# Chunk products of w_ada one at a time, in wider and even intervals, in a diffusion layer on one core

## The chip, the core and the metric

The kernel runs on one core of a Trainium2 chip. The metric is device time in microseconds (us), the median over several executions, less being better. TensorE (PE) multiplies, VectorE (DVE) and ScalarE (ACT) do elementwise work, GpSimd (POOL) helps, and SyncE (SP) issues most of the DMAs. Each engine works through its instructions in the order in which the program hands them over, and waits on semaphores of the others.

## What is computed

One layer of a diffusion backbone with 256 latent tokens, 256 context tokens and a model width of 2048, all in float32. Cut to what matters here:

```python
mod = silu(c) @ w_ada + b_ada          # w_ada is 2048 x 12288
sh_a, sc_a, gt_a, sh_f, sc_f, gt_f = split(mod, 6)
h = rms_norm(x, g_attn) * (1 + sc_a) + sh_a
o = hybrid_mixer(h, hc, w_in, w_out, ...)   # four head groups, one output projection
x = x + gt_a * o
h = rms_norm(x, g_ffn) * (1 + sc_f) + sh_f
x = x + gt_f * swiglu(h, ffn_wg, ffn_wu, ffn_wd)
return rms_norm(x, g_final)
```

The six parts of `mod` are called segments 0 to 5. Segments 0 and 1 (first norm) are needed at the start, segment 2 (gate of the mixer) when the output projection's first sums are added to x, segments 3 and 4 (second norm) after the output projection, and segment 5 (gate of the feed-forward part) late.

## The kernel before, in words

Weights are streamed once, as tiles of 128 rows by 512 columns. `stream_raw` (line 123) issues one DMA on SP for each tile into a ring of eight buffers named raw (`RAW`, line 133). `split` (line 136) makes of each tile two parts whose products TensorE adds: ScalarE casts the upper part (whi, line 142), VectorE subtracts to get the rest (wlo, line 145); each part has a ring of six buffers (`WB`, line 132), that is, three pairs of tiles. `mm3s` (lines 165, 166 and 168) does the three products. A raw buffer is free again when VectorE has read it.

Segments 0 and 1 are multiplied on TensorE (`ada_pe`, line 284; loads on line 203, products on line 301). Segments 2 to 5 go through `ada_block` (line 369): for each block of 512 columns, of which a segment has four, a running sum ada_acc (128 x 512) takes 16 chunks of 128 rows of w_ada. The first is scaled by ScalarE (line 378), each of the others is multiplied by a number of each partition and added by one scalar_tensor_tensor on VectorE (line 380). Then TensorE transposes the sum in four pieces (line 385), and VectorE reduces them to columns and adds the bias (lines 388, 389, for segment 4 also 391): these are called a block's tail. A step of the block handles two chunks; its load is one DMA of two chunks (`ada_raw`, line 279, on SP; `gate_raw`, line 1076, on POOL) or two DMAs into the raw ring that the weights use (`stream_raw`).

What goes between the large products is ordered by a planner written by hand (`Side`, line 32). It has a clock, `now`, in estimated us of TensorE's work, and tasks in lanes. `pump(cost)` is called after each batch of weight products (1.3 for six products of 512 columns, 2.6 for twelve): it moves the clock and lets each lane take the steps that are ready, one a lane and task in a pass, as long as the clock has not moved by more than the cost again. `finish` steps until given tasks are through. The w_ada blocks are the lane "gate", one block at a time; a block's next step is ready at `due`:

```python
due[0] = max(due[0] + gap, side.now - 4 * gap)
yield 0.0, max(0.0, due[0] - side.now)
```

so a late lane may catch up by four steps. The gaps are 7.0 and 3.0 units for two chunks of segment 2 during the w_in stages (lines 547, 550), 3.6 and 2.8 in the attention part (lines 688, 689) and 6.0 for segment 5 (line 1081).

The attention part, from line 688, has in order: projections for two head groups (`proj` pumps 1.3 for each token tile and pair of weight tiles: ML_CQ and DF_Q with two token tiles, 20.8 units each; ML_CKV with four tiles of 320 columns, 26.0; DF_K and DF_V with four, 41.6 each), twelve `attend` heads at 4.36 units each in between, `mla_up` (18.2), evacuations of the projections, and `gq_prep`. Line 933 needs segment 2. The output projection (lines 960 to 970) pumps 2.6 for each of 24 pairs of tiles; the four `diff` heads (6.17 units each, line 890) run beside it. Lines 971 and 972 finish these heads and the blocks of segments 3 and 4; the last quarter of the output projection and the second norm follow.

Of the kernel before, what the change touches and what calls it, by code (L numbers as in the profile page):

```python
# [10 lines left out]
F32 = mybir.dt.float32  # L11
# [6 lines left out]
P = 128  # L18
D = 2048
# [68 lines left out]
def hybrid_dit_kernel(ctx: ExitStack, tc: tile.TileContext, a, out):  # L88
# [187 lines left out]
    scg = const.tile([P, KC, 2], F32, name="scg")  # L276
    sha = const.tile([P, KC, 2], F32, name="sha")

    def ada_raw(src, shape):
        raw = sb0.tile(shape, F32, name="araw", tag="araw", bufs=4)  # L280
        sp.dma_start(raw, src)
        return raw

    def ada_pe(pr, raws=None, per=4, wait=0.0):

# [80 lines left out]

    due = [0.0]

    def ada_block(seg, nb, gap, load, fetched=None):
        c0 = seg * D + nb * 512  # L370
        acc_ = stream.tile([P, 512], F32, name="ada_acc", bufs=2)
        for k2 in range(8):
            raw = fetched(nb, k2) if fetched else load(ada_rows[:, 2 * k2:2 * k2 + 2, c0:c0 + 512], [P, 2, 512])
            for kk in range(2):
                kc = 2 * k2 + kk
                part = raw[kk] if isinstance(raw, list) else raw[:, kk, :]
                if kc == 0:
                    act.activation(acc_, part, AF.Copy, scale=cs[:, 0, 0:1])
                else:
                    dve.scalar_tensor_tensor(out=acc_, in0=part, scalar=cs[:, 0, kc:kc + 1], in1=acc_, op0=ALU.mult, op1=ALU.add)  # L380
            due[0] = max(due[0] + gap, side.now - 4 * gap)
            yield 0.0, max(0.0, due[0] - side.now)
        ps = misc()
        for j in range(4):
            pe.transpose(ps[:, tsl(j)], acc_[:, tsl(j)], ident)  # L385
        k4 = slice(4 * nb, 4 * nb + 4)
        base = colA1 if seg == 4 else colA
        dve.tensor_reduce(out=mcol[seg][:, k4], in_=ps.rearrange("p (j n) -> p j n", j=4), axis=AX.X, op=ALU.add)
        dve.tensor_tensor(out=mcol[seg][:, k4], in0=mcol[seg][:, k4], in1=base[:, seg * 16 + 4 * nb:seg * 16 + 4 * nb + 4], op=ALU.add)
        if seg == 4:  # L390
            dve.tensor_tensor(out=mcol[4][:, k4], in0=mcol[4][:, k4], in1=colB[:, 16 + 4 * nb:20 + 4 * nb], op=ALU.mult)
        yield 0.3, 0.0

    def add_ada(seg, gap, load, nbs=range(4), ahead=0):
        due[0] = side.now
        order = [(nb, k2) for nb in nbs for k2 in range(8)]
        held = {}

        def fetched(nb, k2):

            i = order.index((nb, k2))
            for nb_, k_ in order[i:i + ahead + 1]:
                if (nb_, k_) not in held:
                    c0 = seg * D + nb_ * 512
                    held[nb_, k_] = load(ada_rows[:, 2 * k_:2 * k_ + 2, c0:c0 + 512], [P, 2, 512])
            return held[nb, k2]

        return [side.add(ada_block(seg, nb, gap, load, fetched), lane="gate", width=1) for nb in nbs]

    parts = [[0], [1], [2, 3], [4, 5], [6, 7]]  # L410

# [126 lines left out]
    for gi, prs in enumerate(parts):  # L538
# [5 lines left out]
                    nxt[-1]["ready"] = side.now + 8.0  # L544
        if gi == 2:
            made = prepare()
            gate_tasks = add_ada(2, 7.0, ada_raw, (0, 1))
        if gi == len(parts) - 1:
            keep(*made)
            gate_tasks += add_ada(2, 3.0, ada_raw, (2,))  # L550
        if gi == 0:
            first_group()
        else:
# [131 lines left out]
        pool.dma_start(g, gd.partition_broadcast(P))  # L685
        return g

    gate_tasks = add_ada(2, 3.6, stream_raw, (3,))
    mod_tasks = add_ada(4, 3.6, stream_raw) + add_ada(3, 2.8, stream_raw)

    act.activation(na_qT, na_qT, AF.Copy, scale=128.0 ** -0.5)
    sc_mm = plain_score(na_qT, na_kT, lambda h: h)
# [380 lines left out]

    groups = [(0, 4), (4, 8), (8, 11)]

    def gate_raw(src, shape):
        raw = ff.tile(shape, F32, name="graw", bufs=4)
        pool.dma_start(raw, src)
        return raw

    gate_f = add_ada(5, 6.0, gate_raw, ahead=3)
    gfin = ff.tile([P, D], F32, name="gfin")
    pool.dma_start(gfin, a["g_final"].partition_broadcast(P))
    for gi, (f0, f1) in enumerate(groups):
# [135 lines left out]
```

## Time and profile before

| what | us |
|---|---|
| median of 3 executions | 1363.53 (1361.96 to 1364.54) |
| the profiled execution's own time | 1367.65 |
| its span from the first to the last instruction | 1365.9 |
| TensorE busy in it | 1333.8 (98%) |
| VectorE busy in it | 915.1 (67%) |
| ScalarE busy in it | 624.9 (46%) |

The profile is one execution. A line of a timeline has the start and the length in us, the engine (PE products, PEld weight loads, a "q" for its sequencer), the line of the kernel, the operation, output<-inputs, and a count of like instructions that were merged; in brackets stands how long the engine was idle before it and what released it. A line of waits says who waited for whom, the total in us, the number of times and the longest. A line of windows has, after the stretch and its length, the busy us and the number of instructions of each engine, the granted clock of TensorE as a share of 2.4 GHz, the DMA share and GB/s.

### The profile page before, as it was taken

What the parts mean: (1) busy time and instruction counts of PE and PEld (TensorE: products, weight loads), DVE (VectorE), ACT (ScalarE), POOL (GpSimd) and SP (SyncE); (2) the same over time, 40 slices, a digit from 0 to 9 for tenths busy, and PEclk for the clock granted to TensorE, in tenths of its full rate; (3) what the DMA queues carried; (4) which work ended last, traced back from release to release, by engine and by line L of the source; (5) the groups of instructions that cost most, each with busy time, mean ns of one, the idle gap of its engine ahead of it and who ended that gap; (6) DMA issues with size and microseconds to landing.
All of it is one profiled execution on the core that took longest, in us unless ns stands there. A gap on an engine that the chain in (4) does not pass through costs nothing.

```text
span 1365.9 us, 20914 instructions
## 1 busy us (share of the span) xinstructions
PE 1333.8 (98%) x7082; PEld 1085.5 (79%) x7082; DVE 915.1 (67%) x1623; ACT 624.9 (46%) x1183; POOL 55.0 (4%) x78
## 2 busy tenths in 40 slices
PE   6999999999999999999999999999999999999997
PEld 4788888778876777777888888888888888888886
DVE  4587789988678747878895854445545566555565
ACT  5432243654334435557444444444444444444453
POOL 1100000100000000000220000000000000000000
PEclk9999999999999999999999999999999999999999
DMA  9999997586677756455997755665656665666553
GB/s 367 348 349 330 324 356 215 164 269 205 198 246 261 240 172 213 137 180 163 365 385 262 248 184 192 194 191 188 197 184 190 219 193 186 202 189 191 190 177 131
DMA packets 186687, 313.87 MB, mean 230 GB/s; under 512 B 21171, under 2 KB 61141, under 8 KB 185429
## 3 DMA queue, kind: packets, MB, share of 16 engines
q1 hardware_dynamic: 177568, 285.28, 64.0%
q0 software_dynamic: 5664, 24.14, 4.6%
q10 hardware_dynamic: 3348, 3.13, 0.8%
q8 instruction: 55, 0.90, 0.3%
q14 instruction: 52, 0.42, 0.1%
HBM read 310.36 MB, written 2.11 MB: 229 GB/s over the span
## 4 chain that ended last, share of the span: by engine, by line
PE 68%; DVE 1%; ACT 1%; DMA 0%; issue 0%; POOL 0%; POOLq 0%; DVEq 0%; SPq 0%; ACTq 0%
PE acc L165 21%; PE acc L168 21%; PE acc L166 21%; PE m L1069 1%; PE m L607 1%; PE m L862 1%; PE m L861 1%; PE m L913 1%; PE m L897 1%; PE m L658 1%; PE m L165 0%; PE m L166 0%; PE m L168 0%; ACT whi L142 0%; PE m L385 0%
## 5 line engine op out<-in xcount | busy, mean ns | idle before, releaser
L145 DVE TENSOR_TENSOR wlo<-raw,whi 128x512 fp32r<-128x512 f32 (+1 forms) x764 | 492.1, 681 | 319.5 <-ACT whi L142 314.5
L142 ACT CAST whi<-raw 128x512 fp32r<-128x512 f32 (+1 forms) x764 | 436.8, 615 | 552.5 <-PE acc L166 471.2
L165 PE MATMUL acc<-whi,h_hi 128*128 128x512 f32 x704 | 275.1, 391 | 0.7 <-ACT h_hi L1013 0.7
L166 PE MATMUL acc<-whi,h_lo 128*128 128x512 f32 x704 | 274.2, 390 | 0.4 <-DVE h_lo L1014 0.4
L168 PE MATMUL acc<-wlo,h_hi 128*128 128x512 f32 x704 | 190.7, 390 | 0.1
L165 PE MATMUL acc<-whi,h 128*128 128x512 f32 (+1 forms) x416 | 162.0, 393 | 1.3 <-ACT tok L791 0.5
L166 PE MATMUL acc<-whi,h 128*128 128x512 f32 (+1 forms) x416 | 157.7, 381 | 0.0
L168 PEld LDWEIGHTS acc<-wlo,h_hi 128*128 128x128 f32 x704 | 132.1, 188 | 28.4 <-DVE wlo L145 0.9
L165 PEld LDWEIGHTS acc<-whi,h_hi 128*128 128x128 f32 x704 | 132.2, 188 | 27.9 <-ACT h_hi L1013 1.1
L166 PEld LDWEIGHTS acc<-whi,h_lo 128*128 128x128 f32 x704 | 132.2, 188 | 27.8 <-DVE h_lo L1014 0.7
L165 PE MATMUL acc<-whi,ah 128*128 128x512 f32 (+1 forms) x364 | 139.0, 383 | 0.0
L166 PE MATMUL acc<-whi,al 128*128 128x512 f32 (+1 forms) x364 | 138.6, 382 | 0.0
L168 PE MATMUL acc<-wlo,h 128*128 128x512 f32 (+1 forms) x416 | 115.2, 381 | 2.0 <-DVE wlo L145 1.8
L380 DVE SCALAR_TENSOR_TENSOR ada_acc<-raw,cs,ada_acc 128x512 f32<-128x512 f32 x135 | 101.0, 748 | 22.6 <-DMA raw<-in_w_ada_dram 20.8
L168 PE MATMUL acc<-wlo,ah 128*128 128x512 f32 (+1 forms) x364 | 96.2, 382 | 0.0
L165 PEld LDWEIGHTS acc<-whi,h 128*128 128x128 f32 x416 | 78.3, 189 | 19.6 <-issue 4.0
L168 PEld LDWEIGHTS acc<-wlo,h 128*128 128x128 f32 x416 | 76.0, 188 | 17.8 <-DVE wlo L145 4.1
L166 PEld LDWEIGHTS acc<-whi,h 128*128 128x128 f32 x416 | 78.4, 188 | 13.7 <-issue 1.5
L165 PEld LDWEIGHTS acc<-whi,ah 128*128 128x128 f32 x364 | 68.4, 188 | 13.3
L166 PEld LDWEIGHTS acc<-whi,al 128*128 128x128 f32 x364 | 68.4, 188 | 13.2
L168 PEld LDWEIGHTS acc<-wlo,ah 128*128 128x128 f32 x364 | 67.6, 188 | 13.3
L165 PE MATMUL acc<-whi,o_hi 128*128 128x512 f32 x128 | 51.1, 401 | 1.1 <-ACT whi L142 0.8
(233 smaller groups left out, 1347.9 us busy)
## 6 DMA issues: line engine op xcount, KB each, us to landing
raw<-in_ffn_wg_dram SPq DMA_DIRECT2D x176, 256.0 KB, 2.8
raw<-in_ffn_wu_dram SPq DMA_DIRECT2D x176, 256.0 KB, 2.8
raw<-in_ffn_wd_dram SPq DMA_DIRECT2D x176, 256.0 KB, 3.7
raw<-in_w_in_dram SPq DMA_DIRECT2D x144, 256.0 KB, 4.8
raw<-in_w_ada_dram SPq DMA_DIRECT2D x144, 256.0 KB, 3.5
araw<-in_w_ada_dram SPq DMA_DIRECT2D x128, 256.0 KB, 5.2
raw<-in_w_out_dram SPq DMA_DIRECT2D x64, 256.0 KB, 3.4
graw<-in_w_ada_dram POOLq DMA_DIRECT2D x32, 512.0 KB, 6.4
```

Source lines behind the costliest of these rows:

```text
L142: act.copy(hi, raw_)
L145: dve.tensor_tensor(out=lo, in0=raw_, in1=hi.bitcast(F32), op=ALU.subtract)
L165: pe.matmul(dst, lhsT=l[0], rhs=r[0], start=start, stop=False)
L166: pe.matmul(dst, lhsT=l[0 if w_left else 1], rhs=r[1 if w_left else 0], start=False, stop=False)
L168: pe.matmul(dst, lhsT=l[1 if w_left else 0], rhs=r[0 if w_left else 1], start=False, stop=stop)
L380: dve.scalar_tensor_tensor(out=acc_, in0=part, scalar=cs[:, 0, kc:kc + 1], in1=acc_, op0=ALU.mult, op1=ALU.add)
L607: pe.transpose(ps[:, tsl(j)], src[:, tsl(j)], ident)
L658: pe.matmul(o[:, :S], lhsT=vt(kc)[:, v0:v0 + P], rhs=pT[:, kc, :], start=(kc == 0), stop=(kc == 3))
L861: pe.matmul(sc, lhsT=ml_qT[:, h, tsl(t)], rhs=ml_kT[:, h, :], start=True, stop=False)
L862: pe.matmul(sc, lhsT=qpeT[hb, h // 2, tsl(t)], rhs=kpeT[hb, :], start=False, stop=True)
L897: pe.matmul(sc, lhsT=df_qT[hb, h, tsl(t)], rhs=df_kT[h // 2][hb, h % 2, :], start=True, stop=True)
L913: pe.matmul(o[:, tsl(t)], lhsT=pT[:, kc, tsl(t)], rhs=vt[:, kc, tsl(h)], start=(kc == 0), stop=(kc == 3))
```

## The change

Each step of a block now handles one chunk, and a wait stands between the two chunks of a load as well. The gap is given for each block and for one chunk. Where the old gaps are halved (segment 2 in the w_in stages, segment 5, the last block of segment 2) the mean rate is the old one; segments 4 and 3 go from 3.6 and 2.8 units for two chunks to 2.2 for one. A late lane catches up by one chunk's gap instead of four steps. In the attention part a step loads its one chunk (one DMA, as before); elsewhere the load of two chunks stays. All blocks of that part share one call. The core of the diff:

```diff
-    def ada_block(seg, nb, gap, load, fetched=None):
-        c0 = seg * D + nb * 512
+    def ada_block(seg, nb, gap, fetched, per):
         acc_ = stream.tile([P, 512], F32, name="ada_acc", bufs=2)
-        for k2 in range(8):
-            raw = fetched(nb, k2) if fetched else load(ada_rows[:, 2 * k2:2 * k2 + 2, c0:c0 + 512], [P, 2, 512])
-            for kk in range(2):
-                kc = 2 * k2 + kk
-                part = raw[kk] if isinstance(raw, list) else raw[:, kk, :]
+        for k0 in range(0, KC, per):
+            for kk, part in enumerate(fetched(seg, nb, k0)):
+                kc = k0 + kk
                 if kc == 0:
                     act.activation(acc_, part, AF.Copy, scale=cs[:, 0, 0:1])
                 else:
                     dve.scalar_tensor_tensor(out=acc_, in0=part, scalar=cs[:, 0, kc:kc + 1], in1=acc_, op0=ALU.mult, op1=ALU.add)
-            due[0] = max(due[0] + gap, side.now - 4 * gap)
+                if kk < per - 1:
+                    due[0] = max(due[0] + gap, side.now - gap)
+                    yield 0.0, max(0.0, due[0] - side.now)
+            due[0] = max(due[0] + gap, side.now - gap)
             yield 0.0, max(0.0, due[0] - side.now)
...
-            gate_tasks = add_ada(2, 7.0, ada_raw, (0, 1))
+            gate_tasks = add_ada([(2, 0, 3.5), (2, 1, 3.5)], ada_raw)
...
-            gate_tasks += add_ada(2, 3.0, ada_raw, (2,))
+            gate_tasks += add_ada([(2, 2, 1.5)], ada_raw)
...
-    gate_tasks = add_ada(2, 3.6, stream_raw, (3,))
-    mod_tasks = add_ada(4, 3.6, stream_raw) + add_ada(3, 2.8, stream_raw)
+    def head_raw(src):
+        return stream_raw(src, [P, 1, 512])
+
+    mod_tasks = add_ada([(2, 3, 1.8)] + [(4, nb, 2.2) for nb in range(4)] + [(3, nb, 2.2) for nb in range(4)], head_raw, 1)
+    gate_tasks = mod_tasks[:1]
...
-    gate_f = add_ada(5, 6.0, gate_raw, ahead=3)
+    gate_f = add_ada([(5, nb, 3.0) for nb in range(4)], gate_raw, ahead=3)
```

`add_ada` now takes a list of (segment, block, gap), and `ada_raw` and `gate_raw` hand back the two halves of their tile.

## Rows read from the trace of the kernel before

**Rows 1.** The page's first part: busy us, share of the span, instructions.

```profile
PE 1333.8 (98%) x7082; PEld 1085.5 (79%) x7082; DVE 915.1 (67%) x1623; ACT 624.9 (46%) x1183; POOL 55.0 (4%) x78
```

**Rows 2.** Windows of 25 us (columns as told above).

```profile
225.00:250.00 25.00, 25.00 (x107) 19.35 (x106) 24.36 (x58) 8.58 (x18) 2.25 (x2) 1.00 0.65 193
250.00:275.00 25.00, 25.00 (x126) 19.76 (x125) 23.84 (x62) 17.92 (x39) 3.94 (x4) 1.00 0.60 178
275.00:300.00 25.00, 23.04 (x101) 16.69 (x100) 22.43 (x42) 15.11 (x36) 1.85 (x2) 0.93 0.81 265
300.00:325.00 25.00, 23.34 (x110) 18.07 (x108) 19.73 (x38) 13.15 (x30) 0.00 (x0) 1.00 0.75 242
...
350.00:375.00 25.00, 23.84 (x142) 20.62 (x141) 15.88 (x40) 9.67 (x29) 2.16 (x4) 1.00 0.62 174
375.00:400.00 25.00, 22.97 (x118) 19.23 (x117) 16.70 (x34) 9.14 (x18) 0.00 (x0) 0.93 0.72 220
```

**Rows 3.** Waits from 276 to 291 us: total us, times, longest.

```profile
ACT whi L142 <- DMA raw<-in_w_in_dram: 7.4, 3, 3.2
...
PE m L748 <- ACT gq_kT L742: 1.9, 1, 1.9
```

**Rows 4.** Timeline from 278 to 291 us.

```profile
279.62 3.11 DVE L380 SCALAR_TENSOR_TENSOR ada_acc<-raw,cs,ada_acc 128x512 f32<-128x512 f32 x4
...
284.16 0.93 SPq L128 DMA_DIRECT2D raw<-in_w_in_dram  x2
...
285.62 0.62 ACT L142 CAST whi<-raw 128x512 fp32r<-128x512 f32 x1 [1.14 <-DMA raw<-in_w_in_dram]
286.15 0.47 ACT L742 ACTIVATE gq_kT<-m,colB 128x256 f32<-128x256 f32 x1
...
286.67 3.51 PE L748 MATMUL m<-gq_kT,qT 128*128 128x512 f32 x4 [1.91 <-ACT gq_kT L742]
...
289.19 1.38 PE L166 MATMUL acc<-whi,h 128*128 128x512 f32 x1
...
290.40 0.40 PE L165 MATMUL acc<-whi,h 128*128 128x512 f32 x1
```

**Rows 5.** Timeline of TensorE from 308 to 320 us.

```profile
310.26 1.88 PE L748 MATMUL m<-gq_kT,qT 128*128 128x512 f32 x4
...
317.13 0.63 PE L607 MATMUL m<-ident,p 128*128 128x128 f32 x4 [1.34 <-DVE p L650]
319.45 0.63 PE L607 MATMUL m<-ident,p 128*128 128x128 f32 x4 [0.32 <-DVE p L650]
```

**Rows 6.** Waits from 384 to 394 us.

```profile
ACT whi L142 <- DVE ada_acc L380: 6.2, 1, 6.2
...
PE acc L168 <- DVE wlo L145: 1.8, 1, 1.8
```

**Rows 7.** Waits of SP's DMA queue from 220 to 500 us.

```profile
SPq L128 <- DVE ada_acc L380: 57.1, 102, 3.0
```

**Rows 8.** The tile ada_acc: duration in ns (min/median/max), first and last start in us.

```profile
L380 DVE SCALAR_TENSOR_TENSOR ada_acc<-raw,cs,ada_acc x135: 730/751/756, 222.7 to 486.2; 128x512 f32<-128x512 f32 x135
...
L378 ACT ACTIVATE ada_acc<-raw,cs x9: 712/725/736, 217.7 to 463.8; 128x512 f32<-128x512 f32 x9
...
  DMA raw<-in_w_ada_dram: 26.3, 30
```

**Rows 9.** Windows: two undisturbed ones, and the attention part.

```profile
125.00:150.00 25.00, 25.00 (x239) 20.94 (x238) 20.64 (x42) 7.11 (x13) 0.00 (x0) 1.00 0.94 321
...
875.00:900.00 25.00, 25.00 (x112) 20.71 (x111) 11.77 (x19) 11.41 (x21) 0.00 (x0) 1.00 0.62 194
...
225.00:487.00 262.00, 255.19 (x1230) 201.27 (x1229) 210.49 (x419) 116.69 (x257) 10.21 (x12) 0.99 0.73 227
```

**Rows 10.** Windows: before, during and after the output projection's first three quarters.

```profile
596.00:640.00 44.00, 41.71 (x188) 31.43 (x187) 41.76 (x81) 36.30 (x78) 1.73 (x2) 1.00 0.58 181
...
487.00:507.00 20.00, 20.00 (x92) 16.57 (x91) 6.09 (x11) 6.00 (x11) 0.00 (x0) 1.00 0.39 125
507.00:596.00 89.00, 88.52 (x432) 68.70 (x431) 67.79 (x138) 49.02 (x100) 4.67 (x7) 1.00 0.52 172
```

**Rows 11.** VectorE by line, 507 to 596 us: busy us, mean ns, idle before, releasers.

```profile
L145 DVE TENSOR_TENSOR wlo<-raw,whi 128x512 fp32r<-128x512 f32 x46 | 29.8, 686 | 12.5 <-ACT whi L142 12.3 <-issue 0.2
...
L921 DVE TENSOR_SCALAR tok<-m,rstd 128x128 f32<-128x128 f32 x8 | 2.4, 347 | 3.5 <-POOL rstd L177 2.7 <-PE m L607 0.9
...
L388 DVE TENSOR_REDUCE mcol<-m 128x4 f32<-128x512 f32 x1 | 0.7, 684 | 0.0
...
L389 DVE TENSOR_TENSOR mcol<-mcol,colA 128x4 f32<-128x4 f32 x1 | 0.2, 152 | 0.0
```

**Rows 12.** The w_in stages: a wait of SP, a batch's issue and first use, its landing.

```profile
SPq L203 <- DVE ada_acc L380: 13.1, 12, 2.0
...
135.59 2.42 SPq L203 DMA_DIRECT2D araw<-in_w_ada_dram  x3
...
153.85 1.96 PE L301 MATMUL m<-araw,cs 128*32 128x128 f32 x64
...
araw<-in_w_ada_dram SPq DMA_DIRECT2D x128, 256.0 KB, 5.2
```

**Rows 13.** Segment 5: the window of its products, and the products.

```profile
656.00:774.00 118.00, 118.00 (x538) 97.89 (x537) 101.54 (x160) 56.58 (x100) 20.23 (x28) 1.00 0.89 323
...
L380 DVE SCALAR_TENSOR_TENSOR ada_acc<-graw,cs,ada_acc x60: 739/747/754, 656.9 to 773.6; 128x512 f32<-128x512 f32 x60
```

**Rows 14.** Timeline near 521 us: a softmax row's last step and its transposes.

```profile
520.38 0.75 DVE L905 SCALAR_TENSOR_TENSOR p<-p,st 128x512 f32<-128x512 f32 x1
...
521.06 1.03 PE L607 MATMUL m<-ident,p 128*128 128x128 f32 x8
```

More of the change, by code (lines that the diff above doesn't have):

```diff
@@ L277, in hybrid_dit_kernel, with ada_raw @@
     sha = const.tile([P, KC, 2], F32, name="sha")
-    def ada_raw(src, shape):
-        raw = sb0.tile(shape, F32, name="araw", tag="araw", bufs=4)
+    def ada_raw(src):
+        raw = sb0.tile([P, 2, 512], F32, name="araw", tag="araw", bufs=4)
         sp.dma_start(raw, src)
-        return raw
+        return raw[:, 0, :], raw[:, 1, :]
     def ada_pe(pr, raws=None, per=4, wait=0.0):
@@ L392, in ada_block, with add_ada, fetched @@
         yield 0.3, 0.0
-    def add_ada(seg, gap, load, nbs=range(4), ahead=0):
+    def add_ada(blocks, load, per=2, ahead=0):
         due[0] = side.now
-        order = [(nb, k2) for nb in nbs for k2 in range(8)]
+        order = [(seg, nb, k0) for seg, nb, _ in blocks for k0 in range(0, KC, per)]
         held = {}
[L399 to L408, printed above, removed]
+        def fetched(*at_):
+            i = order.index(at_)
+            for s in order[i:i + ahead + 1]:
+                if s not in held:
+                    seg, nb, k0 = s
+                    c0 = seg * D + nb * 512
+                    held[s] = load(ada_rows[:, k0:k0 + per, c0:c0 + 512])
+            return held[at_]
+        return [side.add(ada_block(seg, nb, gap, fetched, per), lane="gate", width=1) for seg, nb, gap in blocks]
     parts = [[0], [1], [2, 3], [4, 5], [6, 7]]
@@ L1074, in hybrid_dit_kernel, with gate_raw @@
     groups = [(0, 4), (4, 8), (8, 11)]
-    def gate_raw(src, shape):
-        raw = ff.tile(shape, F32, name="graw", bufs=4)
+    def gate_raw(src):
+        raw = ff.tile([P, 2, 512], F32, name="graw", bufs=4)
         pool.dma_start(raw, src)
-        return raw
-    gate_f = add_ada(5, 6.0, gate_raw, ahead=3)
+        return raw[:, 0, :], raw[:, 1, :]
+    gate_f = add_ada([(5, nb, 3.0) for nb in range(4)], gate_raw, ahead=3)
     gfin = ff.tile([P, D], F32, name="gfin")
```

## The prediction

> **What bounds the kernel now.** I read the page first, then windows of 25 us, then the waits, the timeline and the windows of the stages that the edited lane touches. On the page TensorE is busy for 98% of the span and VectorE for 67% [rows 1]; the reader is to see that TensorE is the bound as a whole and that only stretches where its busy time falls below the window can give time back. Matmul ends are modelled, so a full window hides small waits. Where the gate columns of segment 5 are multiplied, from 656 to 774 us, TensorE is busy for 118.00 of 118 us [rows 13], so nothing is to be had there. Among the windows before, three matter [rows 2]: 275 to 300 us (23.04 of 25 busy, clock 0.93), 300 to 325 (23.34) and 375 to 400 (22.97, clock 0.93). A mean of 0.93 is some 3.5 us at the lower of the two levels, which loses half of that, 1.75 us, on top of the wait; what TensorE did just before each fall was to wait for about 2 us.
>
> The waits name the culprits. Near 284 us TensorE stood 1.9 us for gq_kT from ScalarE; ScalarE was late because a weight cast ahead of it waited for a w_in load [rows 3], and the timeline shows why: four chunk products (L380) in a row, 3.11 us, held the raw buffers, and SP issued the weights between w_ada loads that waited for those buffers [rows 4]. The four score matmuls after it took 3.51 us where the same four took 1.88 later, and the next matmul 1.38 where 0.40 is usual [rows 4, 5]: 1.6 + 1.0 us from the low clock. Near 317 us TensorE waited 1.34 and 0.32 us for a softmax row that stood behind chunks in VectorE's queue [rows 5]. Near 392 us it waited 1.8 us for a wlo, whose cast had itself waited 6.2 us for a buffer that a chunk held [rows 6]. Over 220 to 500 us SP waited 102 times, 57.1 us in all, for chunk products [rows 7]. So the lane does delay TensorE, in three places.
>
> **The change, part by part.** The chunk's price stays: 135 products of 0.75 us on VectorE and 9 scalings of 0.72 on ScalarE, all between 217.7 and 486.2 us [rows 8]. The loads stay too: stream_raw already issued one 256 KB DMA per chunk, so neither SP's count nor the bytes change. What moves is when.
>
> *Where the chunks go.* The planner's own costs between lines 688 and 972 add up to 317.5: projections 150.8, out-projection 62.4, twelve attention heads 52.3, mla_up 18.2, four differential heads 24.7, evacuations and gq_prep 6.4, nine block ends 2.7. Before, the lane asks 40 x 3.6 + 32 x 2.8 = 233.6 of it, so it is through before the out-projection (the last 62.4 + 24.7 = 87.1), as the 486.2 shows. After, it asks 16 x 1.8 + 128 x 2.2 = 310.4. At the out-projection's start, at 230.4, 16 + 201.6/2.2 = 107 chunks are out and 37 are left. The intervals are even only as far as the planner's steps of 1.3 to 2.6 and its jumps of some 6 allow, so that up to three chunks still come together; and lateness over two gaps is now lost, so the lane's end slips by several units, to about the end of the out-projection; the last one or two chunks are then emitted by the finish on line 972.
>
> *Gain.* Between 222 and 487 us VectorE gets 37 fewer chunks, 27.8 us less, in single steps. The three places cost 1.9 + 1.6 + 1.0 = 4.5, then 1.7, then 1.8 + 1.75 = 3.6, together 9.8 us [rows 2 to 6]. Bounds: 0 (only fewer chunks come there, so I see nothing that adds a wait) and 9.8. I take 7.5, nearer the top, since in each place the chunks that do the holding come two to four in a row and these rows are denser there than what the new gap allows; some of it will return as shorter waits. The 1.16 us missing between 350 and 375 belong to small evacuations and stay.
>
> One reading rule could make this term larger. The trace counts 6.8 us of missing matmul time from 225 to 487 us, but 201.27 us of weight loading in 262, or 77%, against 20.71 in 25, or 83%, where TensorE runs undisturbed [rows 9]. The Trainium skill (Perfetto Trace Analysis, Identifying the Most-Contended Engine) holds that matmul busy time is a poor measure because matmuls are pipelined, and tells us to judge by the weight loads instead: by that rule up to 19 us could be had here. The attention's 512-column fp32 matmuls load few weights per microsecond, so the waits' 9.8 us are what I count.
>
> *Loss.* The out-projection runs from 507 to 596 us, 89 us for the planner's 87.1. TensorE is busy for 88.52 of it, VectorE for 67.79 [rows 10]. To that come 37 x 0.75 = 27.8 us and two more block tails of 0.68 + 0.15 [rows 11], 1.7 us: 97.2 us of VectorE work in a stage of 89. That is 8.2 too many. Waits for rstd from GpSimd, 2.7 us, stand in VectorE's order and cannot be filled [rows 11], so 10.9. The 14 us that VectorE idles between 487 and 507 [rows 10] don't help: the first reduction of each differential head waits for scores that TensorE reaches at 507, and the chunks stand behind it. What helps: wlo buffers for three pairs, 6 x 29.8/46 = 3.9 us of VectorE's work [rows 11], are a lead that it may use up. But the stage after needs that lead: from 596 to 640 us VectorE is busy for 41.76 of 44 [rows 10], so only 2.2 us are absorbed for good. 10.9 - 2.2 = 8.7, and one fall of the clock at 1.75 makes 10.5 us. Bounds: 0, because from 225 to 275 us VectorE was busy for 24.36 and 23.84 of 25 with TensorE full [rows 2], and 17: 97.2 us at the 95% that the stage after reaches is 102.4, 13.4 over, and two falls of the clock. I take 10.5, because the demand is over 100% and not only near it. A chunk may also wait for its own load, 26.3 us over 30 cases in this lane [rows 8]; where VectorE is behind, the load has landed, so I count nothing, and the cover gone it would be 37 x 30/144 x 0.88, about 7 us, inside the upper bound with the lead used up.
>
> *Gates of segment 2 during the w_in stages, and segment 5.* Cost nothing. The second half of an araw tile is now used half an interval later, so a ring slot is held up to 3.5 units longer, and SP, which waits there already (13.1 us in 12 cases [rows 12]), issues ada_load's tiles and the w_in weights queued behind them later. The cover: a batch issued from 135.59 us is first used at 153.85 [rows 12], some 18 us on, with a landing of 5.2, and the windows are full with all of it in place [rows 9]. If that cover went, each batch would cost TensorE up to 3.5 us. Segment 5 hides under 118.00 of 118 us [rows 13]; its last product is at 773.6 and its rows are wanted in the second group's evacuations, so POOL's queue has slack.
>
> Sum: -7.5 + 10.5 = +3.0 us on the profiled execution's 1367.65, 1370.7. That execution is 4.1 above the median of 1363.53, so the median becomes 1366.5.
>
> **The rivals.** *Room in the out-projection* (not slower): the chunks fall into VectorE's 21.2 idle us there, much of it waits for a cast that itself waits for TensorE (12.3 us of ScalarE's making [rows 11]), and the lead covers the rest, loss 2 us. For it: full windows at 97% load near 240 us. Against: demand over 100%, and at 521 us the softmax row that TensorE transposes is finished only as it gets there [rows 14], so one chunk ahead of it is seen at once. -7.5 + 2 = -5.5, 1358. It decides from where the added work is under the idle that can be used.
>
> *Hidden either way*: the three waits reappear from another source (casts, loads) and the out-projection copes; both terms near 2, the time stays, 1363.5. For it: VectorE was above 95% near 270 us without a loss. Against: the named waits end on chunks.
>
> *Late hand-over* (slower): the last block's transposes are emitted by line 972, ahead of the remaining w_out products in TensorE's order, and must wait for the last chunk on a VectorE that is behind by its whole excess; the norm that follows has no slack. The full excess, 13.4, plus two falls of the clock is 17; with 4 of gain, +13, 1376.5. It decides from an excess of about the lead, 4 us, at the stage's end.
>
> **How the numbers follow.** About 0.2%, 2.7 us, is what a measurement of this kernel can tell from no change. The forecast gets 0.47, of which 0.33 lies above +2.7 and 0.14 within; the first rival 0.28 (0.25 faster, 0.03 within), the second 0.13 (0.10 within, 0.03 faster), the third 0.12, slower. Faster 0.28, same 0.27, slower 0.45. Own range of the forecast: 1362 to 1372. The range of 8 in 10 goes from 1356 (gain 9.8, loss 2) to 1376.5 (the third rival).
>
> **What would show it.** Right: chunk products lie between 218 and about 600 us; the windows 275 to 300 and 375 to 400 are full at clock 1.00; VectorE is near 100% from 510 to 595, TensorE there waits for wlo or a softmax row, and the out-projection ends about 10 us later relative to its start. Wrong: no wait of TensorE on VectorE in the out-projection and a stage of 89 to 91 us, then the kernel is faster; or the waits near 284, 317 and 392 us still there, then slower by more than forecast. Segment 2 or 5 is misjudged if TensorE waits for araw or the page shows late gate rows.

## The result, and the profile after

The kernel after takes 1376.32 us, the median of four executions (1373.23 to 1378.16), beside 1363.72 us for the kernel before on the same chip: a ratio of 1.0087 [1.0070, 1.0104], slower. The forecast was 1366.5, so the sign is right and the size is not: 12.6 us were lost where 3.0 were forecast. The profiled execution has a span of 1376.2 us, 10.3 more than before; that of before took 1367.65 us, 3.9 above its median, that of after 1378.03, 1.7 above its own, so the profiles show 2.2 us less of the loss than the medians do.

The page's first part [rows 1] now reads:

```profile
PE 1338.0 (97%) x7082; PEld 1087.3 (79%) x7082; DVE 910.4 (66%) x1623; ACT 625.2 (45%) x1183; POOL 55.2 (4%) x78
```

The counts of instructions are the same. TensorE's busy time is 4.2 us more for them, the rest of the 10.3 is waiting. To see where, cut each trace at three matmuls: the first scores of the attention part (m<-kT,qT), the first scores of the differential heads (m<-df_kT,qT, where the output projection begins), and the first product of h_hi (line 165, after the second norm). Times in us; the kernels e1 to e12 are those of the next section, the column of chunks counts products and first scalings that start after the out-projection does, and the last one is of the chunk products of the attention part's lane on VectorE:

```
kernel  attention part        out-projection   rest   chunks after     VectorE idle
        from   to     length  length                  its start        before chunks
before  244.3  507.3  263.0   115.1            743.5   0               21.0
after   246.3  505.1  258.8   127.6            743.5  30               54.2
e1      244.7  509.4  264.7   123.5            744.1   6               52.8
e2      246.1  508.5  262.4   125.1            743.6  26               49.6
e3      246.4  499.5  253.1   121.5            743.5  16                0
e4      245.6  504.4  258.8   125.6            743.6  27               56.2
e5      244.6  498.9  254.3   115.0            743.4   0                0
e6      245.6  509.7  264.1   125.6            743.8  28               56.5
e7      251.5  508.8  257.3   136.6            742.8  20               48.5
e8      245.1  504.1  259.0   115.1            743.8   0               22.5
e9      248.2  505.1  256.9   128.0            743.4   -                0
e10     248.8  519.3  270.4   115.4            744.0   0               25.0
e11     245.7  513.9  268.1   115.4            743.7   0               33.6
e12     248.7  500.8  252.1   124.9            743.4   -                0
```

The attention part is 4.2 us shorter, the out-projection 12.5 longer, and the rest is the same; 2.0 us more lie before the attention part, where executions differ anyway (the thirteen runs of before beside e12 range from 1362.95 to 1368.32).

Some of both numbers is work that changed its stage. With 30 chunks the transposes of three blocks' tails came into the out-projection. Lines of TensorE and of VectorE in the kernel after, 505 to 608 us (busy us, mean ns, idle before):

```profile
L385 PE MATMUL m<-ident,ada_acc 128*128 128x128 f32 x12 | 1.8, 271 | 0.0
```

```profile
L377 DVE SCALAR_TENSOR_TENSOR ada_acc<-raw,cs,ada_acc 128x512 f32<-128x512 f32 x29 | 21.6, 744 | 5.7 <-DMA raw<-in_w_ada_dram 5.7
```

In the kernel before all 36 of these transposes lie in the attention part. Without the 1.8 us that moved, 2.4 are won and 10.7 lost. The loss is well clear of noise: the out-projection takes 115.0 to 115.4 us in all five kernels that have no chunk in it, and 121.5 to 136.6 in all others. The gain isn't: it rests on one execution of each kernel, that of before was a long one, and e8, whose median is that of the kernel before, has an attention part of 259.0.

Windows of the kernel after, with the columns of [rows 2, 10, 13]:

```profile
275.00:300.00 25.00, 23.15 (x109) 17.19 (x107) 23.14 (x44) 16.56 (x38) 1.42 (x2) 1.00 0.83 272
300.00:325.00 25.00, 24.27 (x112) 18.93 (x113) 17.00 (x33) 12.18 (x28) 0.00 (x0) 1.00 0.61 191
350.00:375.00 25.00, 22.50 (x123) 19.14 (x123) 15.23 (x40) 9.28 (x28) 2.54 (x4) 0.93 0.51 146
375.00:400.00 25.00, 25.00 (x145) 21.99 (x145) 16.16 (x31) 8.93 (x18) 0.00 (x0) 1.00 0.70 217
...
505.00:608.00 103.00, 96.08 (x450) 73.33 (x449) 88.10 (x173) 52.52 (x106) 5.40 (x7) 0.98 0.69 228
656.00:774.00 118.00, 118.00 (x534) 97.82 (x533) 93.99 (x148) 54.67 (x96) 23.70 (x33) 1.00 0.89 326
```

Of the three places of [rows 2], the window from 375 is full, and that from 300 misses 0.7 us instead of 1.7. From 275 to 300 us the clock is 1.00, but TensorE still misses 1.85 us, where it was 1.96: the wait for gq_kT is gone, and two others of 0.67 and 0.94 us came. The window from 350, which had lost 1.16 us of TensorE's time, now loses 2.5 and stands at clock 0.93. In the out-projection TensorE misses 6.9 of 103 us, and VectorE is busy for 88.10 of 103, or 86%: it is not full.

The tile ada_acc, whose rows answer to [rows 8] (the last row: idle time of its engines before it, us and times):

```profile
L377 DVE SCALAR_TENSOR_TENSOR ada_acc<-raw,cs,ada_acc x135: 727/750/755, 224.7 to 597.1; 128x512 f32<-128x512 f32 x135
...
  DMA raw<-in_w_ada_dram: 70.4, 49
```

A product costs what it did (750 ns), but VectorE and ScalarE now stand 70.4 us in 49 cases waiting for a chunk to land, where it was 26.3 in 30. Most of it lies in the attention part; of VectorE's share 5.7 us are in the out-projection (the line of L377 above). The timeline of the kernel after near 359 us shows what one such wait does:

```profile
351.98 0.54 SPq L824 DMA_DIRECT2D raw<-in_mla_wuq_dram  x1
352.58 1.08 SPq L128 DMA_DIRECT2D raw<-in_w_ada_dram  x2
...
356.98 0.75 DVE L377 SCALAR_TENSOR_TENSOR ada_acc<-raw,cs,ada_acc 128x512 f32<-128x512 f32 x1 [3.82 <-DMA raw<-in_w_ada_dram]
...
361.12 0.48 DVE L790 SCALAR_TENSOR_TENSOR tok<-acc,rstd,b_mla_gkv 128x256 f32<-128x256 f32 x1 [0.72 <-POOL rstd L177]
...
361.65 0.69 PE L609 MATMUL m<-ident,tok 128*128 128x128 f32 x2 [2.29 <-DVE tok L790]
```

SP issues the chunk's load behind weights, 4.4 us before its use; VectorE stands 3.82 us ahead of the chunk and then works without a pause through what was queued up behind it, a block's tail and a second chunk among it, before it gets to the next tokens' evacuation; TensorE waits 2.29 us for those tokens (0.31 at this place in e3, which has no chunk loads), and then runs a stretch at the lower of its two levels (the 0.93 of that window). The same happens in the out-projection near 588 us:

```profile
583.12 0.37 SPq L128 DMA_DIRECT2D raw<-in_w_ada_dram  x1
584.82 0.75 DVE L377 SCALAR_TENSOR_TENSOR ada_acc<-raw,cs,ada_acc 128x512 f32<-128x512 f32 x1 [3.34 <-DMA raw<-in_w_ada_dram]
...
590.57 0.59 PE L609 MATMUL m<-ident,tok 128*128 128x128 f32 x2 [1.85 <-DVE tok L926]
```

The costliest wait there has no chunk's load right before it. TensorE and VectorE near 534 us:

```profile
530.92 0.74 DVE L377 SCALAR_TENSOR_TENSOR ada_acc<-raw,cs,ada_acc 128x512 f32<-128x512 f32 x1
...
533.90 0.68 DVE L961 TENSOR_TENSOR tm<-acc,gate 128x512 f32<-128x512 f32 x1
...
534.57 0.67 DVE L145 TENSOR_TENSOR wlo<-raw,whi 128x512 fp32r<-128x512 f32 x1
...
536.23 0.68 DVE L145 TENSOR_TENSOR wlo<-raw,whi 128x512 fp32r<-128x512 f32 x1
536.83 0.74 DVE L910 SCALAR_TENSOR_TENSOR p<-p,st 128x512 f32<-128x512 f32 x1
...
537.72 0.63 PE L609 MATMUL m<-ident,p 128*128 128x128 f32 x4 [3.43 <-DVE p L910]
```

VectorE works without a pause from 528 to 540 us, on chunks, casts, residual sums and softmax rows in program order; the row that TensorE transposes next comes behind all of it, 3.43 us late, and a second fall of the clock follows.

### The profile page after: what moved, and what is told of

It reads as the page before. It is cut to its first block, busy times and chain, and to the rows that moved or that the text cites. A ratio compares the mean times of both kernels' runs of the same rounds, so it can differ in the third digit from the quotient of the medians.

```text
span 1376.2 us, 20896 instructions
## 1 busy us (share of the span) xinstructions
PE 1338.0 (97%) x7082; PEld 1087.3 (79%) x7082; DVE 910.4 (66%) x1623; ACT 625.2 (45%) x1183; POOL 55.2 (4%) x78
## 4 chain that ended last, share of the span: by engine, by line
PE 80%; DVE 9%; DMA 6%; issue 2%; ACT 2%; POOL 1%; SPq 0%; ACTq 0%; DVEq 0%; POOLq 0%
PE acc L165 24%; PE acc L168 24%; PE acc L166 24%; DMA raw<-in_w_ada_dram 3%; DVE wlo L145 2%; DVE ada_acc L377 2%; PE m L301 2%; DMA araw<-in_w_ada_dram 1%; DVE st L636 1%; POOL rstd L177 1%; PE m L268 1%; PE m L1074 1%; PE m L609 1%; ACT whi L142 1%; PE m L660 1%
## 5 line engine op out<-in xcount | busy, mean ns | idle before, releaser
L377 DVE SCALAR_TENSOR_TENSOR ada_acc<-raw,cs,ada_acc 128x512 f32<-128x512 f32 x135 | 100.9, 747 | 55.5 <-DMA raw<-in_w_ada_dram 52.7
```

## The experiments

Unless said otherwise each was timed against the kernel before on the same chip, and its edit is against the kernel after. The stage table above holds all their profiled executions.

**e1: the old rate in single, even steps.**

```diff
-    mod_tasks = add_ada([(2, 3, 1.8)] + [(4, nb, 2.2) for nb in range(4)] + [(3, nb, 2.2) for nb in range(4)], head_raw, 1)
+    mod_tasks = add_ada([(2, 3, 1.8)] + [(4, nb, 1.8) for nb in range(4)] + [(3, nb, 1.4) for nb in range(4)], head_raw, 1)
```

> The changed kernel with the old mean intervals in the attention part: 1.8 units a chunk for segment 4 and 1.4 for segment 3 in place of 2.2; single steps, single loads and the one-chunk catch-up stay. By the planner's clock 13 chunks are left when the output projection starts, against 37 in the changed kernel and none before. Theory A (chunks moved into the output projection cost TensorE there, since VectorE has no slack): the stage returns to about 91 us from 103 and the time to 1364 to 1367. Theory B (a chunk loaded alone, in step with its use, makes VectorE wait for its own load, wherever it stands): those waits stay near the changed kernel's 70 us and the time stays above 1370. Theory C (catching up by one chunk only): above 1370 as well, since the catch-up is unchanged.

Measured 1384.61 us, 1.0143 [1.0117, 1.0170]; its profiled execution, 1378.82 us, was the quickest of its runs, so the table shows the smaller part of its loss. Even single steps at the old rate win nothing in the attention part (264.7 us), and although only 6 chunks are left after its start the out-projection takes 123.5. The loss sits at its head, in the timeline of e1:

```profile
507.14 1.54 DVE L377 SCALAR_TENSOR_TENSOR ada_acc<-raw,cs,ada_acc 128x512 f32<-128x512 f32 x2 [2.90 <-DMA raw<-in_w_ada_dram]
...
512.03 1.12 PE L902 MATMUL m<-df_kT,qT 64*128 64x512 f32 x2 [1.47 <-DVE mcol L388]
513.98 0.75 DVE L377 SCALAR_TENSOR_TENSOR ada_acc<-raw,cs,ada_acc 128x512 f32<-128x512 f32 x1 [2.00 <-DMA raw<-in_w_ada_dram]
...
518.40 0.80 PE L166 MATMUL acc<-whi,o_lo 128*128 128x512 f32 x1 [2.09 <-DVE o_lo L952]
```

Two steps of the lane wait for their own loads ahead of work that TensorE needs. So the number of chunks in the out-projection does not set the loss by itself. Theory A failed (1364 to 1367); B and C both gave such a time. As the rate is the old one, the whole loss of e1 comes with single steps, single loads and the short catch-up.

**e2: the kernel before (chunks in pairs), at the new mean rate.**

```diff
-    mod_tasks = add_ada(4, 3.6, stream_raw) + add_ada(3, 2.8, stream_raw)
+    mod_tasks = add_ada(4, 4.4, stream_raw) + add_ada(3, 4.4, stream_raw)
```

> The kernel before with only the wider interval: 4.4 units for two chunks in segments 4 and 3 (3.6 and 2.8 before); two chunks a step, two loads a step and the catch-up of four steps stay. 34 chunks are then left at the start of the output projection. Theory A: about as slow as the changed kernel, 1372 to 1380. Theory B: 1362 to 1367, since loads still come in twos and the second chunk finds its data there. Theory C: 1362 to 1367.

Measured 1376.98 us, 1.0093 [1.0078, 1.0109], the time of the kernel after within the intervals. Theory A holds: the wider gap alone makes a loss of this size, and at this gap single steps and the shorter catch-up change little (an attention part of 258.8 against 262.4, a difference that single executions can make). At the old rate they do cost, as e1 shows and e10 and e11 show again.

**e3 and e5: no chunk loads, in the kernel after and in the kernel before.** One tile is loaded once and every chunk product of the attention part reads it. e3:

```diff
+    hraw = const.tile([P, 512], F32, name="hraw")
+    sp.dma_start(hraw, ada_rows[:, 0, 4 * D:4 * D + 512])
...
     def head_raw(src):
-        return stream_raw(src, [P, 1, 512])
+        return [hraw]
```

> The changed kernel with the loads of segments 2 (last block), 4 and 3 in the attention part left out: one chunk of w_ada is loaded once into a tile of its own and every product there takes it. All products, their order and their intervals stay; 143 DMAs of 256 KB and their places in the raw ring are gone, so these segments are not what the reference has. Theory B: the output projection's stage falls to 90 to 93 us and the time to 1357 to 1365. Theory A: VectorE's work there is unchanged, the stage stays at 98 us or more and the time above 1370.

Measured 1365.55 us, 1.0002 [0.9992, 1.0012]. e5 does the same to the kernel before (`head_raw` gives `[hraw, hraw]` to its three add_ada calls):

> The kernel before with the chunk loads of the attention part left out, as in the run without chunk loads of the changed kernel: one chunk is loaded once and every product of segments 2 (last block), 4 and 3 there takes it, so these are not the reference's; products, pairs, intervals and catch-up are as before. It is the fair partner of that run. Theory A (VectorE's work in the output projection is what costs): this kernel keeps its lead over that run, 8 us or more: 1353 to 1358. Theory B (the chunks' own loads are what costs, through the ring and SP's queue): both kernels lose the loads' harm, and what is left between them is under 4 us: 1360 to 1365.

Measured 1359.15 us, 0.9962 [0.9951, 0.9973]. The four kernels make a square:

```
                     chunks as before   chunks as after   difference
with their loads     1363.72            1376.32           +12.6
without loads        1359.15            1365.55            +6.4
the loads cost          4.6               10.8
```

Both results lie between the theories. About half of the loss is there without any load: products that moved. The other half goes with their loads, which cost 4.6 us in the old places and 10.8 in the new. The medians of the square come from different chips; by the ratios to the kernel before on the same chip the products cost 5.5 us (e3 against e5) and the loads 5.2 and 11.6, so the split stands to about 1 us. The same split shows in the out-projection: 115.0 (e5), 121.5 (e3, of which the moved transposes are 1.8), 127.6 (after). A window of each over it, up to about 25 us before its end, e5 first and e3 second:

```profile
498.90:588.00 89.10, 88.62 (x430) 68.95 (x430) 67.87 (x139) 49.02 (x100) 4.68 (x7) 1.00 0.53 172
```

```profile
499.50:596.00 96.50, 94.33 (x447) 72.89 (x447) 79.51 (x158) 52.19 (x105) 5.53 (x7) 0.98 0.49 159
```

In e3 VectorE is busy for 79.51 of 96.50 us, and still TensorE misses 2.2 us and loses some to the clock (0.98): even without loads the added products delay by their place in VectorE's order, with 18% of its time free.

One reservation holds for the whole square. The program is put in order by its builder after the planner, and an edit that takes loads away changes the order of other instructions too. At the softmax row near 534 us the kernel after has nothing between the two groups of transposes, e3 has three products there. TensorE, the kernel after first and e3 second:

```profile
533.70 0.60 PE L609 MATMUL m<-ident,p 128*128 128x128 f32 x4
537.72 0.63 PE L609 MATMUL m<-ident,p 128*128 128x128 f32 x4 [3.43 <-DVE p L910]
```

```profile
528.04 0.60 PE L609 MATMUL m<-ident,p 128*128 128x128 f32 x4
528.39 0.48 PE L165 MATMUL acc<-whi,o_hi 128*128 128x512 f32 x1
...
530.30 0.66 PE L609 MATMUL m<-ident,p 128*128 128x128 f32 x4 [0.96 <-DVE p L913]
```

So the 3.43 us are 0.96 without the loads, and part of that difference is the other order. How much of the 11 us that go with the loads is their waits, and how much the order that they bring about, no run separates.

**e4: catch-up of eight gaps** for the lane with single chunks (the same in both lines that set `due`).

```diff
-            due[0] = max(due[0] + gap, side.now - gap)
+            due[0] = max(due[0] + gap, side.now - (8 if per == 1 else 1) * gap)
```

> The changed kernel with the old catch-up in the attention part: a late lane may catch up by eight chunks (four steps of two, as before) in place of one. The wider single intervals stay; 35 chunks are left at the start of the output projection, and the lane is through 11 units before its end instead of after it. Theory C: most of the loss goes, 1363 to 1368. Theories A and B: 1372 to 1379, as only the last chunk's hand-over is gone, 1 to 2 us.

Measured 1375.11 us, 1.0077 [1.0060, 1.0093], not to be told from the kernel after: 27 chunks stay behind instead of 30. At this gap the shorter catch-up is a detail; theory C failed.

**e6 and e7: loads issued earlier.** e6 fetches two chunks ahead (`head_raw, 1, 2`). e7 does so from a ring of three of its own, with six raw buffers for the weights:

```diff
-    RAW = 8
+    RAW = 6
...
-        return stream_raw(src, [P, 1, 512])
+        raw = stream.tile([P, 512], F32, name="hraw", bufs=3)
+        sp.dma_start(raw, src[:, 0])
+        return [raw]
```

> The changed kernel with each chunk's load handed to SP two chunks earlier (still in the weights' ring of eight); products, intervals and catch-up unchanged. Theory B: VectorE's waits for chunk loads in the attention part fall from 70 us to under 30 and the time to 1362 to 1369. Theory A: the waits may fall, but the output projection stays near 103 us and the time above 1372. A third possibility: chunks that lie in the ring two steps longer leave it too short for the weights, and the time rises above 1378.

> The changed kernel with a ring of three tiles for the chunks of the attention part, loaded two chunks ahead, and six raw tiles (in place of eight) for the weights everywhere. Theory B: a chunk's load no longer waits for a weight's slot, though it still stands in SP's order; its waits fall to under 25 us and the time to 1360 to 1368, if six raw tiles are enough for the weights (seen in the feed-forward stages, where nothing else changes). Theory A: above 1372.

e6 measured 1378.75 us, 1.0107 [1.0089, 1.0124], e7 1390.18, 1.0176 [1.0145, 1.0207], over three executions; a fourth took 6397.15 us, for a reason that is not known, and is left out. VectorE still stands 56.5 and 48.5 us before chunks. Asking for a load earlier in program order doesn't bring it earlier: it waits at its place in SP's order for a buffer, and the weights behind it wait too. In e7 SP's queue waits longest, from 225 to 640 us, for these rows (as [rows 7]):

```profile
SPq L128 <- DVE wlo L145: 128.3, 122, 13.8
SPq L692 <- DVE ada_acc L377: 65.5, 94, 5.1
SPq L692 <- DMA hraw<-in_w_ada_dram: 31.3, 30, 5.1
```

In the kernel after the first two are 121.2 in 134 cases and 63.1 in 97. The chunks' own ring did not free SP of the products, and TensorE was the worse for it (136.6 us of out-projection). The weights have two buffers fewer in e7, and what those cost here was not tried by itself; in the rest, 742.8 us, they cost nothing.

**e8: one step ahead in the kernel before** (`ahead=1` for segments 4 and 3).

> The kernel before with the loads of segments 4 and 3 handed to SP one step (two chunks) ahead; everything else as before. Theory B: the waits of VectorE for chunk loads, 26 us before, fall, and the three places near 284, 317 and 392 us cost less, since the weights' loads there no longer follow a late chunk load: 1355 to 1362. If the ring is the limit and not the moment of the load: 1364 or slower. Theory A says nothing of it: 1361 to 1366.

Measured 1365.15 us, 1.0003 [0.9993, 1.0014]. No difference in the old places either: the time is that of the ring as the limit.

**e9: the loads without the products.**

```diff
-                else:
+                elif per == 2:
                     dve.scalar_tensor_tensor(out=acc_, in0=part, scalar=cs[:, 0, kc:kc + 1], in1=acc_, op0=ALU.mult, op1=ALU.add)
```

> The changed kernel with the chunk products of the attention part left out (segments 2, last block, 4 and 3: only each block's first chunk is scaled, so these segments are not the reference's); all 144 loads keep their order and intervals in SP's queue and in the raw ring. It shows what the loads cost by themselves (ring, SP's order, DMA). Theory B1 (a load costs only because VectorE stands in order before its product): time 1350 to 1360 and an output projection of 115 us from the first score product to the first feed-forward product. Theory B2 (the loads make the weights late): that stage stays above 119 us and the time above 1360.

Measured 1377.24 us, 1.0095 [1.0074, 1.0116]: as slow as the kernel after, with no product in VectorE's order. The first scaling of each block is left, on ScalarE, and the longest wait stands before one of them. Timeline of e9:

```profile
546.73 4.91 SPq L128 DMA_DIRECT2D raw<-in_w_ada_dram  x3
550.57 0.72 ACT L375 ACTIVATE ada_acc<-raw,cs 128x512 f32<-128x512 f32 x1 [6.21 <-DMA raw<-in_w_ada_dram]
...
552.74 3.92 PE L902 MATMUL m<-df_kT,qT 64*128 64x512 f32 x4 [4.57 <-ACT oT L928]
```

ScalarE stands 6.21 us for the chunk, the copy of an output row (oT) behind it comes late, and TensorE waits 4.57 us; from 549 to 560 us its granted clock is 0.53 on the mean, where 0.50 is the lower of its two levels. Of the 12.9 us that e9 loses in the out-projection, these scalings' waits are 3.1 at most: e12 takes them away and keeps 9.8.

**e10 and e11: all chunks before the out-projection, evenly.** Both take e4's catch-up of eight; e10 sets every gap to 1.5, e11 to 1.6 with two loads a step (`stream_raw(src, [P, 2, 512])`, single products).

> The changed kernel with 1.5 units a chunk for all nine blocks of the attention part and the old catch-up of eight chunks: single products and loads in even intervals, denser than before in segment 4 (1.8) and wider than in none but through at 414 on the planner's clock, 18 before the output projection. Theory A+B (what costs is a chunk, with or without its load, in the output projection): that stage is back at 115 to 117 us, the attention part at 258 to 266 us, the time at 1360 to 1368. If single steps cost by themselves: 1370 or more, with the loss in the attention part.

> Like the run with 1.5 units, but with two loads a step as before, single products at 1.6 units, and a catch-up of eight; the lane is through at 428, 4 before the output projection. If the moment of the load matters in the attention part (every second product finds its chunk landed): the attention part is 2 to 5 us shorter than with single loads and the time 1358 to 1365. If not: as the run with 1.5 units, within 2 us.

e10 measured 1379.22 us, 1.0095 [1.0065, 1.0124], e11 1374.32, 1.0069 [1.0054, 1.0084]. The out-projection is back at 115.4 us in both, and the attention part pays instead: 270.4 and 268.1. The place is the same as at 359 us above; timeline of e11:

```profile
358.29 1.08 SPq L128 DMA_DIRECT2D raw<-in_w_ada_dram  x2
363.20 0.75 DVE L377 SCALAR_TENSOR_TENSOR ada_acc<-raw,cs,ada_acc 128x512 f32<-128x512 f32 x1 [4.70 <-DMA raw<-in_w_ada_dram]
...
367.89 0.47 PE L609 MATMUL m<-ident,tok 128*128 128x128 f32 x1 [5.63 <-DVE tok L790]
```

Neither beats the kernel before. Both expectations of a gain failed: at a rate near the old one, with no chunk left behind, single steps cost by themselves, 9 to 13 us. Two loads a step are quicker by 2.3 us in the attention part and by 4.9 between the medians, less than is lost.

**e12: all loads, and nothing that waits for them.**

```diff
+    hraw = const.tile([P, 512], F32, name="hraw")
...
-                    act.activation(acc_, part, AF.Copy, scale=cs[:, 0, 0:1])
-                else:
+                    act.activation(acc_, hraw if per == 1 else part, AF.Copy, scale=cs[:, 0, 0:1])
+                elif per == 2:
```

> The kernel after, with all 144 chunk loads in their places and their order, but with nothing in the attention part that waits for them. Left out: the products of w_ada there (the last block of segment 2, segments 4 and 3), of which only each block's first scaling stays, and that reads one fixed chunk; a buffer is free again as soon as its load has landed. Theory B1 (a load costs only through the engine that stands in order before its use): no fall of the clock after the first 100 us, the out-projection 115 to 117 us, the time 1355 to 1361. Theory B2 (the loads make the weights late by themselves, through SyncE's order and the DMA engines): the out-projection stays over 119 us and the time over 1366.

Measured 1368.04 us, 1.0020 [1.0006, 1.0034]. The numbers are those of B2: the out-projection takes 124.9 us, 9.8 more than before (1.8 of it the moved transposes), with no chunk product on VectorE and no engine standing for a chunk. From 500 to 630 us SP and ScalarE waited so:

```profile
SPq L128 <- DMA raw<-in_w_ada_dram: 53.6, 28, 5.4
...
ACT whi L142 <- DMA raw<-in_w_out_dram: 14.2, 9, 3.3
```

In the kernel before SP has no wait of the first kind there, and the second is 2.4 us in 3 cases. A load whose buffer last held a chunk is issued only when that chunk has landed, and the weights behind it in SP's order wait too; so casts come late, and with them what stands behind the casts. But this isn't what the kernel after does. Its rows for the same stretch are:

```profile
SPq L128 <- DVE ada_acc L377: 9.3, 17, 1.0
SPq L128 <- DMA raw<-in_w_ada_dram: 5.3, 4, 2.1
...
ACT whi L142 <- DMA raw<-in_w_out_dram: 7.2, 7, 2.5
```

The ring gives a buffer away again as soon as nothing later in the program reads it, and in e12 nothing reads a chunk. Of the 37 chunk loads between the first and the last load of w_out, 22 pass their buffer to the second load after them in e12's program and 7 in the kernel after's. e12 thus shows that loads beside the weights can cost this stage up to 8.0 us with no engine in their way; what they cost by themselves in the kernel after it doesn't show. The nearest number for that is after against e3, 6.1 us, with the reservation above. In e9, too, SP stands 50.8 us in 28 cases for the landing of chunks. Timeline of e12:

```profile
536.17 0.86 SPq L128 DMA_DIRECT2D raw<-in_w_out_dram  x2
537.34 0.62 ACT L142 CAST whi<-raw 128x512 fp32r<-128x512 f32 x1 [2.11 <-DMA raw<-in_w_out_dram]
...
537.99 0.69 DVE L145 TENSOR_TENSOR wlo<-raw,whi 128x512 fp32r<-128x512 f32 x1 [3.00 <-ACT whi L142]
...
541.62 0.58 PE L611 MATMUL m<-ident,tok 128*128 128x128 f32 x2 [1.11 <-DVE tok L928]
...
546.51 2.07 PE L904 MATMUL m<-df_kT,qT 64*128 64x512 f32 x2 [1.06 <-ACT p L640]
```

In the attention part, on the other hand, the same kernel takes 252.1 us, the shortest of all: there the loads by themselves cost nothing that shows, though SP stands 116.1 us in 88 cases for them from 249 to 500 us. That what they cost there comes through the engine that stands for them is likely, not shown. Why the two parts differ is open.

## Why the prediction was right in sign and wrong in size

The measured 1376.32 us lies 0.2 below the upper end of the range, 1376.5, an end that stood for the third rival; the forecast's own range ended at 1372. That the range holds the result is luck, since that rival's mechanism did not come.

*Where the chunks go*: 30 were left at the out-projection's start where 37 were forecast, and the last product began at 597.1 us, at the stage's end as said. The planner's arithmetic is a fair guide.

*Gain*: 2.4 us measured without the moved transposes, at the edge of what one execution of each can tell; 7.5 taken. This is the term that was mis-sized: with the transposes taken out of both terms, 5.1 of the 5.3 us by which the two stages miss the forecast are here. The places near 284 and 392 us went, that near 317 shrank to 0.64 us. What came back was a wait that I had ruled out with "I see nothing that adds a wait": near 359 us a chunk's own load (2.29 us and a fall of the clock), and smaller waits near 297 us (0.94, for a softmax row on ScalarE) and near 455 (1.06, for a copy on ScalarE) whose origin stays open. Single steps were to spare the three places, and they did not: with them at the old rate the part takes 264.7 us (e1), 270.4 (e10) and 268.1 (e11), not less than before. The size of the whole was well read: without chunk loads, all products in place (e5), the part takes 254.3, that is 8.7 less than before, against the 9.8 that the three places added up to; with no chunk in any engine's way (e12) it is 252.1, 10.9 less, of which 1.8 are the transposes. The Trainium skill (Perfetto Trace Analysis, Identifying the Most-Contended Engine) tells us to judge TensorE's headroom by the weight loads' share rather than by its busy time. The estimate of up to 19 us made from that share did not come true; no run gave back more than 9.1.

*Loss*: 12.5 us measured, 10.7 without the moved transposes, which the forecast put at nothing in both terms; 10.5 taken. That these two agree is luck, for the reason failed. The step was "because the demand is over 100% and not only near it": VectorE is busy for 88.10 of 103 us where 97.2 of work were counted, and in e3, where no load disturbs it, for 79.51 of 96.50. It was never the bound as a whole. Products moved there cost 6.5 us (e3 against e5): 1.8 for the transposes, the rest by their place in its order, ahead of softmax rows and tokens that TensorE needs next, with a clock fall. The second failed step is "where VectorE is behind, the load has landed, so I count nothing". VectorE isn't behind all the time, SP issues chunk loads only 1.7 to 4.9 us before their use in the rows above, and in e12 loads in this place delay the weights as well. On top of the products the loads go with 6.1 us (after against e3), close to the "about 7 us" that the forecast named and left out.

*The sum*: 4.2 won and 12.5 lost make +8.3 where +3.0 stood; with the 2.0 us before the attention part it is the 10.3 of the spans, and 12.6 between the medians, because the profiled execution of before was further above its median than that of after. A typical execution of before may thus have a shorter attention part than 263.0, and a gain there may not exist. That the change made the 2.0 us no run shows.

*Segment 2 in the w_in stages and segment 5*: for segment 5 as forecast, 118.00 of 118 us still busy, and the rest after the out-projection is 743.5 us in both. For segment 2 no wait for araw is to be seen that would make up the 2.0 us. The new steps there were not tried by themselves, but the table compares them: the kernels with the old w_in stages (before, e2, e5, e8) come to the attention part at 244.3 to 246.1 us, those with the new ones at 244.7 to 248.8 (251.5 with six raw buffers, e7), so a cost of up to some 2 us is neither shown nor ruled out.

*The rivals*: Late hand-over gave the number that came, 1376.5, by a mechanism that did not. TensorE waits nowhere between 591 and 609 us, where the last block's transposes are, and the rest is no longer. Room in the out-projection fell: VectorE's idle time was there, yet no use. Hidden either way fell with it. Of what was to show the forecast, the chunks up to some 600 us, the full window from 375, the clock of 1.00 in both windows and the waits for softmax rows came; a full window from 275 and VectorE near 100% did not.

What stays open, besides the difference of the two parts in e12 and the share of the changed order: a way to take the 4.6 us of the loads (e5) without leaving them out. Issuing them earlier on SP, with or without buffers of their own, did not do it, and no version here beats the kernel before.

## What to carry to other kernels

Side work that moves into another stage needs room in every order that it passes: ahead of which step of its engine it stands, and for its loads ahead of which weights on the issuing queue and in which ring. An engine with a sixth of its time free can still be late when it matters. Single, even steps are not better by themselves: here they lost at the old rate. To price such work, take out its loads and its products one at a time, in the old place and in the new: here that square showed two halves where the totals had suggested one full engine. Then look at what else such a cut changes, such as the order of other instructions or how soon a buffer is given away, before a difference is called the price of one thing.

## What was not expected of the hardware

TensorE's wait of 1.85 us near 589 us left the window from 575 to 600 us at clock 1.00, while the wait of 2.29 us near 360 was followed by a stretch at the lower level (0.93 from 350 to 375), as were waits of 1.91 and 1.82 us in the kernel before (0.93 from 275 to 300 and from 375 to 400). So the length of the last wait alone does not tell. In e12 the fall came at 546 us after no wait over 1.11 us, behind three such waits within 6 us (1.11, 0.72 and 1.06); the granted clock is 0.51 from 546 to 553. Three chunk loads issued together took SP 4.91 us in e9, waits for their buffers included.
